# One triangular inverse for both halves of a macro step: 128 partitions on VectorE instead of 64 on VectorE and 64 on GpSimd

## The chip, the core and the metric

The kernel runs on one core of a Trainium2 chip. The metric is the device time of one execution in microseconds (us), as the median of several runs. Engines are named as the profile names them: PE (TensorE matmul), PEld (its weight load), DVE (VectorE), ACT (ScalarE), POOL (GpSimd), SP (SyncE, which issues most DMAs).

## The reference

One encoder layer is applied to a group of 512 tokens and a group of 1024 tokens: a SwiGLU feed-forward, a mixer, a second SwiGLU feed-forward, each with RMS norms and modulation. The mixer is half a pooling mixer and half a two-directional RWKV-7 scan:

```python
def swiglu(h, w1, w3, w2):
    return (jax.nn.silu(h @ w1) * (h @ w3)) @ w2
...
    def step(S, inp):
        r_t, w_t, k_t, v_t, na_t, b_t = inp
        sa = jnp.einsum('bhvk,bhk->bhv', S, na_t)
        S = S * w_t[:, :, None, :] + sa[..., None] * b_t[:, :, None, :] + v_t[..., None] * k_t[:, :, None, :]
        y = jnp.einsum('bhvk,bhk->bhv', S, r_t)
        return S, y
...
    z = h @ w_in
    m = jnp.concatenate([pool_mixer(zp, pool_w, pool_scale),
                         rwkv7_mixer(zr, w0, w2, a0, a2, g2, k_k, k_a, r_k, lnx_g, lnx_b)], axis=-1)
    m = m.astype(x.dtype) @ w_out
```

There are 8 heads of 64 and two directions. `sa` makes each token depend on the tokens before it, so a chunk of 64 tokens needs the inverse of a unit triangular 64x64 matrix.

## The kernel before, in words

**Main stream.** Tokens go in three blocks of 512. Every large product is made of float32r matmuls of 128x128 by 128x512 on a high and a low half of both operands, three matmuls for one product (`mm3`, line 739: `whi` with `hh`, `whi` with `hl`, `wlo` with `hh`). These 11520 matmuls are called dense below. ACT makes `whi` from the loaded weights, POOL (or DVE, by a rule on how busy they are) makes `wlo` (`WStream.split`, line 495). DVE adds the partial outputs of a feed-forward (`y<-y,y`, line 905). After a feed-forward or an output product, `post_gen` (line 771) and `prenorm` (line 658) run on DVE, ACT and POOL before the same block's next dense matmuls can start. The order of the stages is `mainA`, `mainB`, `mainC` (line 1513).

**Scan.** The heads go in pairs. A macro step (12 in all) covers, for one pair, two halves `gi` = 0 and 1; a half holds 4 chunks of 64 tokens in each of 2 directions for 2 heads, so 16 matrices of 64x64. The macro steps 0 to 7 are of the large group, 8 to 11 of the small one. Four kinds of generators run beside the main stream:

- `scan_prep` (line 1158) makes a half's operands, group after group: tanh and exponentials, the products `AR` and `cs` (BK), transposes, and the matrices `MU` (written by two `mask` multiplications a direction, line 1274). Before it writes a half's `AR` it waits until the state of that half of the last macro step is through (line 1248). It then sets `("ba", m, gi)`.
- `scan_inv` (line 1283) inverts the 16 matrices of a half. Their 32x32 diagonal blocks are turned by two transposes so that a partition holds the rows of one parity of one block (`Tin` below: `XN<-MU`), which takes 64 partitions for a half. A chain of 62 dependent multiply and add operations (`XN<-XN`, lines 1307 to 1309) inverts them, on DVE for half 0 and on POOL for half 1 (line 1292). Two transposes put them back (`Tout`: `MU<-XN`), a third copies a block (`Txg`: `MU<-MU`), all on DVE. The off-diagonal block comes from the join: 16 matmuls of 32x32 into PSUM, a copy on ACT, 16 more and another copy (lines 1318 to 1326). The profile counts each of these matmuls twice. A token, `take("inv")`, lets one half in at a time.
- `scan_state` (line 1331), one for each direction, goes through the 8 chunks of a macro step once `("inv", m, gi)` is set for their half; a chunk is three visits to PE with ACT, POOL (`s0p`) and DVE (`SBD`) between.
- `scan_post` (line 1398) normalises the outputs and writes the mixer's half of `m`.

**What sets the order.** All of it is emitted by `run_until` (line 217), a planner that keeps an estimated clock for each engine (`Estimate`, line 42, with a fixed cost for each kind of operation), asks the generator of lowest `prio` that is ready (inverse and preparation -0.5, state 0, post 0.8, main stream 3), and so writes one fixed sequence for each engine. On the chip each engine goes through its own sequence in order: PE waits where an operand is later than the planner thought. The output product of block 0 needs all macro steps of the large group (`("m", 1)`); the output products of blocks 1 and 2 stand in the second feed-forward of block 0, before its chunk 7 (`OUT_AT`, line 934), and need all macro steps.

Nearly all instructions carry line 161, the recorder's, so the profile is read by tiles.

Of the kernel before, what the change touches and what calls it, by code (L numbers as in the profile page):

```python
# [17 lines left out]
P = 128  # L18
# [4 lines left out]
TB = 512  # L23
# [149 lines left out]
def encoder_kernel(ctx, tc, x_prompt, x_sample, c_prompt, c_sample, ada_w, ada_b, n1_pre, n1_post,  # L173
# [392 lines left out]
    def give(k):  # L566
        held.remove(k)
# [712 lines left out]
            ld = nld  # L1280
            flags.add(("ba", m, gi))

    def scan_inv(sb, gi):


        rows = slice(64 * gi, 64 * gi + 64)
        MA, N0, XS = sb.MA, sb.XN[rows, 0:32, :], sb.XN[rows, 32:48, :]
        tmp = sb.XN[rows, 48:53, :].rearrange("p t s -> p (t s)")
        two = lambda ap: ap.rearrange("p t (a s) -> p t a s", a=2)
        e_ = eyes[rows, 30:31]  # L1290
        eye = bass.AP(tensor=e_.tensor, offset=e_.offset, ap=[list(e_.ap[0]), [-2, 16], [1, 32]])
        E = (V, G)[gi]
        for m in range(len(macros)):
            yield has(("ba", m, gi))
            yield from take("inv")
            U = slice(gi * 16, gi * 16 + 16)
            XG = sb.MU[0:64, 2, U, 0:32]
            diag = [MA[32 * q:32 * q + 32, U, 32 * q:32 * q + 32].rearrange("p u t -> p t u") for q in range(2)]
            S.activation(XS, eye, AF.Copy)
            for q in range(2):  # L1300
                V.transpose(two(N0[32 * q:32 * q + 32]), diag[q].unsqueeze(2).to_broadcast([32, 32, 2, 16]))
            yield WAIT
            for j in range(31, 0, -1):
                lo = j // 2
                k_ = 16 - lo
                t3 = tmp[:, 0:k_ * j].rearrange("p (t s) -> p t s", s=j)
                E.tensor_tensor(t3, N0[:, j:j + 1, 0:j].to_broadcast([64, k_, j]),
                                XS[:, lo:16, j:j + 1].to_broadcast([64, k_, j]), ALU.mult)
                E.tensor_tensor(XS[:, lo:16, 0:j], XS[:, lo:16, 0:j], t3, ALU.add)
                if j % 3 == 1:  # L1310
                    yield CHAIN
            for q in range(2):
                V.transpose(diag[q].rearrange("p (t a) u -> p t a u", a=2), two(XS[32 * q:32 * q + 32]))
            V.transpose(XG[0:32], MA[0:32, U, 0:32])
            yield WAIT
            yield from banks()
            pg = pt([P, TB], "sM", 2, pool=ps)
            for u in range(16):
                mm(pg[32:64, u * 32:u * 32 + 32], MA[0:32, gi * 16 + u, 32:64], XG[0:32, u, :])
            S.activation(XG[32:64], pg[32:64, :].rearrange("p (u i) -> p u i", i=32), AF.Copy)  # L1320
            yield WAIT
            yield from banks()
            pe = pt([P, TB], "sM", 2, pool=ps)
            for u in range(16):
                mm(pe[0:32, u * 32:u * 32 + 32], XG[32:64, u, :], MA[32:64, gi * 16 + u, 32:64])
            S.activation(MA[0:32, U, 32:64], pe[0:32, :].rearrange("p (u i) -> p u i", i=32), AF.Copy)
            yield WAIT
            flags.add(("inv", m, gi))
            give("inv")
# [250 lines left out]
    with tc.tile_pool(name="late", bufs=1, reuse_waits="tile") as lp:  # L1580
        sb = ScanBufs(lp)

        spawn(scan_state(sb, 0), 0)
        spawn(scan_state(sb, 1), 0)
        spawn(scan_inv(sb, 0), PRIO_INV)
        spawn(scan_inv(sb, 1), PRIO_INV)
# [39 lines left out]
```

## Time and profile before

| what | value |
|---|---|
| median of 3 runs | 3867.81 us (3865.55 to 3870.64) |
| the profiled execution | 3878.62 us |
| its span, first to last instruction | 3876.6 us |
| PE busy, mean granted clock | 3649.0 us, 94%; 0.936 |
| DVE / ACT / POOL busy | 1977.2 / 1364.7 / 1704.0 us |
| first and last instruction of an inverse chain | 1210.9 us (DVE), 2775.4 us (POOL) |

The page gives the busy share of each engine in 40 slices, and the clock that was granted to PE (PEclk, 9 is full or nearly). A row of the windows view has the stretch, its length, then for PE, PEld, DVE, ACT and POOL the busy us and the number of instructions, then the granted clock as a share of full, the DMA share and GB/s. A row of the lines view has operation, tiles, shapes and count, then busy us and mean ns, then the idle time of the engine before these instructions and who ended it. A row of the timeline has start, length, operation and, in brackets, the idle time before it and who ended that.

### The profile page before, as it was taken

The page shows a single profiled execution, that of the slowest core. Times are in us where ns is not written, and L with a number is a line of the kernel's source. Part 1 is how long each engine was busy: PE and PEld are TensorE (multiplying, and loading weights), DVE is VectorE, ACT ScalarE, POOL GpSimd, SP SyncE. Part 2 cuts the span into 40 slices and gives each one's busy share as a digit, 9 for nine tenths or more (in the row PEclk, how much of TensorE's full clock was granted, in tenths as well). Part 3 has the DMA queues.
Part 4 walks back from the last instruction along what each step waited for, and adds up shares of the span by engine and source line. Part 5 has one row for each costly group of instructions (what it writes and reads, how often), then busy time and mean ns, then how long its engine had stood idle before and what let it go on. Part 6 is the DMA issues. An engine that isn't in the chain of part 4 may idle for free. (4 is left out here: it accounts for less than half of the span.)

```text
span 3876.6 us, 53921 instructions
## 1 busy us (share of the span) xinstructions
PE 3649.0 (94%) x19579; PEld 2752.9 (71%) x19579; DVE 1977.2 (51%) x3633; ACT 1364.7 (35%) x2592; POOL 1704.0 (44%) x2068
## 2 busy tenths in 40 slices
PE   7999999998999999999889988899999999999998
PEld 4667778876776667666667666566777778877886
DVE  3127352245247557765876676766348632232223
ACT  3324342234444333333334333333234432233222
POOL 2334444442233554355445355445544344444444
PEclk8999999999999989999879787789999999999999
DMA  7655343333443222222324233222245343334332
GB/s 270 238 177 160 98 144 93 98 108 117 128 135 112 63 77 66 74 71 88 120 67 121 84 115 109 88 74 71 64 136 163 102 130 98 95 98 138 94 98 76
DMA packets 557981, 432.11 MB, mean 111 GB/s; under 512 B 27029, under 2 KB 511572, under 8 KB 553620
## 3 DMA queue, kind: packets, MB, share of 16 engines
q1 hardware_dynamic: 524900, 379.90, 32.2%
q10 hardware_dynamic: 32816, 48.78, 4.0%
q8 instruction: 154, 2.52, 0.3%
q14 instruction: 111, 0.91, 0.1%
HBM read 367.23 MB, written 61.34 MB: 111 GB/s over the span
## 5 line engine op out<-in xcount | busy, mean ns | idle before, releaser
L161 POOL TENSOR_TENSOR wlo<-wraw,whi 128x512 fp32r<-128x512 f32 x863 | 1146.3, 1343 | 1778.1 <-ACT whi L161 1259.2
L161 DVE TENSOR_TENSOR y<-y,y 128x512 f32<-128x512 f32 x480 | 327.8, 685 | 870.5 <-PE y L161 869.3
L161 ACT ACTIVATE whi<-wraw 128x512 fp32r<-128x512 f32 x938 | 559.6, 622 | 185.5 <-PE v L161 136.9
L161 PE MATMUL u<-hh,whi 128*128 128x512 f32 x1392 | 571.0, 410 | 12.6 <-ACT hh L161 4.4
L161 PE MATMUL v<-hh,whi 128*128 128x512 f32 x1392 | 571.8, 411 | 8.3 <-ACT zraw L161 4.2
L161 PE MATMUL u<-hl,whi 128*128 128x512 f32 x1392 | 568.0, 408 | 12.1 <-DVE hl L161 10.9
L161 PE MATMUL v<-hl,whi 128*128 128x512 f32 x1392 | 568.6, 408 | 5.1 <-DVE hl L161 5.1
L161 PE MATMUL v<-hh,wlo 128*128 128x512 f32 x1392 | 571.1, 410 | 0.0
L161 PE MATMUL u<-hh,wlo 128*128 128x512 f32 x1392 | 569.8, 409 | 0.1
L161 PE MATMUL y<-gh,whi 128*128 128x512 f32 x1056 | 429.2, 406 | 12.0 <-DVE y L161 10.5
L161 PE MATMUL y<-gl,whi 128*128 128x512 f32 x1056 | 426.9, 404 | 0.0
L161 PE MATMUL y<-gh,wlo 128*128 128x512 f32 x1056 | 425.6, 403 | 0.0
L161 POOL TENSOR_TENSOR XN<-XN 64x126 f32<-64x126 f32 (+22 forms) x744 | 311.3, 418 | 66.1 <-DVE XN L161 8.1
L161 PEld LDWEIGHTS u<-hl,whi 128*128 128x128 f32 x1392 | 268.6, 193 | 83.7 <-DVE hl L161 17.9
L161 PEld LDWEIGHTS u<-hh,whi 128*128 128x128 f32 x1392 | 268.4, 193 | 82.6 <-issue 8.3
L161 PEld LDWEIGHTS v<-hh,whi 128*128 128x128 f32 x1392 | 269.8, 194 | 76.4 <-ACT hh L161 7.1
L161 PEld LDWEIGHTS v<-hl,whi 128*128 128x128 f32 x1392 | 270.1, 194 | 72.5 <-DVE hl L161 8.8
L161 PEld LDWEIGHTS u<-hh,wlo 128*128 128x128 f32 x1392 | 268.9, 193 | 69.6 <-issue 10.1
L161 PEld LDWEIGHTS v<-hh,wlo 128*128 128x128 f32 x1392 | 270.0, 194 | 67.3 <-issue 5.9
L161 ACT ACTIVATE gh<-s 128x512 fp32r<-128x512 f32 x132 | 83.3, 631 | 636.7 <-DVE s L161 636.4
L161 PEld LDWEIGHTS y<-gh,whi 128*128 128x128 f32 x1056 | 202.3, 192 | 67.1 <-DVE y L161 11.7
L161 DVE TENSOR_TENSOR XN<-XN 64x126 f32<-64x126 f32 (+22 forms) x744 | 233.2, 313 | 23.8
(252 smaller groups left out, 4456.3 us busy)
## 6 DMA issues: line engine op xcount, KB each, us to landing
wraw<-in_f_w_dram SPq DMA_DIRECT2D x792, 256.0 KB
ada<-in_ada_w_dram SPq DMA_DIRECT2D x32, 1024.0 KB
wraw<-in_w_in_dram SPq DMA_DIRECT2D x98, 256.0 KB
xk<-xs ACTq DMA_DIRECT2D x96, 256.0 KB
xs<-y ACTq DMA_DIRECT2D x48, 256.0 KB
wraw<-in_w_out_dram SPq DMA_DIRECT2D x48, 256.0 KB
in_k<-zk SPq DMA_DIRECT2D x48, 128.0 KB
in_kk<-zkk SPq DMA_DIRECT2D x48, 128.0 KB
```

Source lines behind the costliest of these rows:

```text
L161: return f(*args, **kw)
```

## The change

`scan_inv` becomes one generator for both halves. Half 0's input transposes are issued when half 0 is prepared, half 1's when half 1 is; one chain of 62 operations then runs on all 128 partitions on DVE; six transposes follow; the joins of both halves are issued together, and each half's flag is set behind its second set of matmuls. The token is gone. The number of instructions of the chain on DVE stays 744 (now of 128 partitions), POOL loses its 744, and PE's matmuls are the same.

```diff
-    def scan_inv(sb, gi):
-        rows = slice(64 * gi, 64 * gi + 64)
+    def scan_inv(sb):
...
-        E = (V, G)[gi]
...
         for m in range(len(macros)):
-            yield has(("ba", m, gi))
-            yield from take("inv")
+            yield has(("ba", m, 0))
             S.activation(XS, eye, AF.Copy)
-            for q in range(2):
-                V.transpose(two(N0[32 * q:32 * q + 32]), diag[q].unsqueeze(2).to_broadcast([32, 32, 2, 16]))
+            for gi in range(2):
+                yield has(("ba", m, gi))
+                for q in range(2):
+                    V.transpose(two(N0[quad(gi, q)]), diag[gi][q].unsqueeze(2).to_broadcast([32, 32, 2, 16]))
             yield WAIT
             for j in range(31, 0, -1):
...
-                E.tensor_tensor(t3, N0[:, j:j + 1, 0:j].to_broadcast([64, k_, j]),
-                                XS[:, lo:16, j:j + 1].to_broadcast([64, k_, j]), ALU.mult)
-                E.tensor_tensor(XS[:, lo:16, 0:j], XS[:, lo:16, 0:j], t3, ALU.add)
+                V.tensor_tensor(t3, N0[:, j:j + 1, 0:j].to_broadcast([P, k_, j]),
+                                XS[:, lo:16, j:j + 1].to_broadcast([P, k_, j]), ALU.mult)
+                V.tensor_tensor(XS[:, lo:16, 0:j], XS[:, lo:16, 0:j], t3, ALU.add)
...
+            for gi in range(2):
+                for q in range(2):
+                    V.transpose(diag[gi][q].rearrange("p (t a) u -> p t a u", a=2), two(XS[quad(gi, q)]))
+                V.transpose(XG[gi][0:32], MA[0:32, U[gi], 0:32])
             yield WAIT
-            yield from banks()
-            pg = pt([P, TB], "sM", 2, pool=ps)
+            yield from banks(2)
+            pj = [pt([P, TB], "sM", 2, pool=ps) for gi in range(2)]
+            for gi, pg in enumerate(pj):
...
             yield WAIT
-            yield from banks()
-            pe = pt([P, TB], "sM", 2, pool=ps)
+            for gi, pe in enumerate(pj):
...
+                yield CHAIN
+                flags.add(("inv", m, gi))
```

The planner's sequences move with it. On PE before, in the first feed-forward of block 2 at macro step 1, this is the join of half 0 (`sM<-MU` rows; `u` and `y` rows are dense, `in_wa` rows belong to the preparation of a later group):

```order
L161 MATMUL u_10801<-hl_8857,whi_10662 128x512
L161 MATMUL sM_10863<-MU_9075 32x32 x16
L161 MATMUL u_10801<-hh_8856,wlo_10663 128x512
L161 MATMUL u_10801<-hh_8856,whi_10662 128x512
L161 MATMUL u_10801<-hl_8857,whi_10662 128x512
L161 MATMUL u_10801<-hh_8856,wlo_10663 128x512
L161 MATMUL sM_10888<-in_wa_10767,w2s_151 128x256
L161 MATMUL sM_10889<-in_wa_10767,w2s_151 128x256
L161 MATMUL y_10894<-gh_10423,whi_10724 128x512
L161 MATMUL sM_10896<-MU_9075 32x32 x16
```

A second such join, of half 1, follows 226 rows later. On PE now, at macro step 1 of the same feed-forward, the first matmuls of both halves stand next to each other:

```order
L161 MATMUL v_11104<-hh_8728,whi_11031 128x512
L161 MATMUL sM_11106<-MU_9075 32x32 x16
L161 MATMUL sM_11107<-MU_9075 32x32 x16
L161 MATMUL v_11104<-hl_8729,whi_11031 128x512
L161 MATMUL v_11104<-hh_8728,wlo_11032 128x512
L161 MATMUL v_11104<-hh_8728,whi_11031 128x512
L161 MATMUL v_11104<-hl_8729,whi_11031 128x512
L161 MATMUL v_11104<-hh_8728,wlo_11032 128x512
L161 MATMUL v_11104<-hh_8728,whi_11031 128x512
L161 MATMUL sM_11106<-MU_9075 32x32 x16
```

Half 1's second set stands four rows further on, and the state of the macro step begins right behind it: two places a macro step at which PE meets a join, where there were four.

On DVE before, this is the end of half 0's chain at macro step 1 (`XN<-XN`), its transposes back, and then the preparation of half 1 and half 1's input transposes:

```order
L161 TENSOR_TENSOR XN_9076<-XN_9076 64x16 x2
L161 TENSOR_TENSOR y_9330<-y_9330,y_10748 128x512
L161 TENSOR_TENSOR s_10615<-s_10615,v_10623 128x512
L161 TENSOR_TENSOR gl_10792<-s_10615,gh_10791 128x512
L161 STREAM_TRANSPOSE MU_9075<-XN_9076 32x32x16 x2
L161 STREAM_TRANSPOSE MU_9075<-MU_9075 32x16x32
L161 TENSOR_TENSOR wlo_10836<-wraw_10621,whi_10835 128x512
L161 TENSOR_TENSOR MU_9075<-sM_10846,mask_88 128x4x2x64
L161 TENSOR_TENSOR MU_9075<-sM_10847,mask_88 128x4x2x64
L161 TENSOR_TENSOR y_9330<-y_9330,y_10841 128x512
L161 STREAM_TRANSPOSE XN_9076<-MU_9075 32x1024 x2
```

On DVE now, the end of the one chain of macro step 1; both halves' six transposes stand together and the state's `SBD` follows:

```order
L161 TENSOR_TENSOR XN_9076<-XN_9076 128x16 x2
L161 TENSOR_TENSOR y_9330<-y_9330,y_11012 128x512
L161 TENSOR_TENSOR s_10941<-s_10941,v_10949 128x512
L161 TENSOR_TENSOR gl_11028<-s_10941,gh_11027 128x512
L161 STREAM_TRANSPOSE MU_9075<-XN_9076 32x32x16 x2
L161 STREAM_TRANSPOSE MU_9075<-MU_9075 32x16x32
L161 STREAM_TRANSPOSE MU_9075<-XN_9076 32x32x16 x2
L161 STREAM_TRANSPOSE MU_9075<-MU_9075 32x16x32
L161 TENSOR_TENSOR y_9330<-y_9330,y_11074 128x512
L161 TENSOR_TENSOR y_9330<-y_9330,y_11088 128x512
L161 SCALAR_TENSOR_TENSOR SBD_9077<-sb_9080,PL_9079,s0p_11189 64x64 x2
```

Before, the chain's rows had `SBD` rows of the state between them; now the state's rows stand in front of the chain and behind it.

More of the change, by code (lines that the diff above doesn't have):

```diff
@@ L1281, in scan_prep @@
             flags.add(("ba", m, gi))
-    def scan_inv(sb, gi):
-        rows = slice(64 * gi, 64 * gi + 64)
-        MA, N0, XS = sb.MA, sb.XN[rows, 0:32, :], sb.XN[rows, 32:48, :]
-        tmp = sb.XN[rows, 48:53, :].rearrange("p t s -> p (t s)")
+    def scan_inv(sb):
+        MA, N0, XS = sb.MA, sb.XN[:, 0:32, :], sb.XN[:, 32:48, :]
+        tmp = sb.XN[:, 48:53, :].rearrange("p t s -> p (t s)")
         two = lambda ap: ap.rearrange("p t (a s) -> p t a s", a=2)
-        e_ = eyes[rows, 30:31]
+        e_ = eyes[:, 30:31]
         eye = bass.AP(tensor=e_.tensor, offset=e_.offset, ap=[list(e_.ap[0]), [-2, 16], [1, 32]])
-        E = (V, G)[gi]
-        for m in range(len(macros)):
-            yield has(("ba", m, gi))
-            yield from take("inv")
-            U = slice(gi * 16, gi * 16 + 16)
-            XG = sb.MU[0:64, 2, U, 0:32]
-            diag = [MA[32 * q:32 * q + 32, U, 32 * q:32 * q + 32].rearrange("p u t -> p t u") for q in range(2)]
+        U = [slice(gi * 16, gi * 16 + 16) for gi in range(2)]
+        XG = [sb.MU[0:64, 2, U[gi], 0:32] for gi in range(2)]
+        diag = [[MA[32 * q:32 * q + 32, U[gi], 32 * q:32 * q + 32].rearrange("p u t -> p t u") for q in range(2)]
+                for gi in range(2)]
+        quad = lambda gi, q: slice(64 * gi + 32 * q, 64 * gi + 32 * q + 32)
+        for m in range(len(macros)):
+            yield has(("ba", m, 0))
             S.activation(XS, eye, AF.Copy)
-            for q in range(2):
-                V.transpose(two(N0[32 * q:32 * q + 32]), diag[q].unsqueeze(2).to_broadcast([32, 32, 2, 16]))
+            for gi in range(2):
+                yield has(("ba", m, gi))
+                for q in range(2):
+                    V.transpose(two(N0[quad(gi, q)]), diag[gi][q].unsqueeze(2).to_broadcast([32, 32, 2, 16]))
             yield WAIT
@@ L1310, in scan_inv @@
+                V.tensor_tensor(XS[:, lo:16, 0:j], XS[:, lo:16, 0:j], t3, ALU.add)
                 if j % 3 == 1:
                     yield CHAIN
-            for q in range(2):
-                V.transpose(diag[q].rearrange("p (t a) u -> p t a u", a=2), two(XS[32 * q:32 * q + 32]))
-            V.transpose(XG[0:32], MA[0:32, U, 0:32])
+            for gi in range(2):
+                for q in range(2):
+                    V.transpose(diag[gi][q].rearrange("p (t a) u -> p t a u", a=2), two(XS[quad(gi, q)]))
+                V.transpose(XG[gi][0:32], MA[0:32, U[gi], 0:32])
@@ L1326, in scan_inv @@
[L1326 to L1329, printed above, removed]
+            yield from banks(2)
+            pj = [pt([P, TB], "sM", 2, pool=ps) for gi in range(2)]
+            for gi, pg in enumerate(pj):
+                for u in range(16):
+                    mm(pg[32:64, u * 32:u * 32 + 32], MA[0:32, gi * 16 + u, 32:64], XG[gi][0:32, u, :])
+                S.activation(XG[gi][32:64], pg[32:64, :].rearrange("p (u i) -> p u i", i=32), AF.Copy)
@@ L1331, in scan_state @@
+            yield WAIT
+            for gi, pe in enumerate(pj):
+                for u in range(16):
+                    mm(pe[0:32, u * 32:u * 32 + 32], XG[gi][32:64, u, :], MA[32:64, gi * 16 + u, 32:64])
+                S.activation(MA[0:32, U[gi], 32:64], pe[0:32, :].rearrange("p (u i) -> p u i", i=32), AF.Copy)
+                yield CHAIN
+                flags.add(("inv", m, gi))
     def scan_state(sb, d):
```

8 lines of the change are left out of this document (1 added, 7 removed).

## The prediction

> **What bounds the kernel now.** I read the page first, then the windows view by stage, then the waits of PE, then the timeline around the joins, and last the lines view for the prices.
>
> ```profile
> PE 3649.0 (94%) x19579; PEld 2752.9 (71%) x19579; DVE 1977.2 (51%) x3633; ACT 1364.7 (35%) x2592; POOL 1704.0 (44%) x2068
> ```
>
> PE is the bound: no other engine is busy for more than half of the span. The time is PE's work, plus its idle time, plus what it loses to a lowered clock. The windows view gives the last two by stage (the last row is a stretch of the second feed-forward without scan):
>
> ```profile
> 1200.00:1900.00 700.00, 659.59 (x4471) 473.35 (x4471) 475.48 (x1010) 243.03 (x522) 337.38 (x539) 0.92 0.26 76
> 1900.00:2520.00 620.00, 550.76 (x3653) 390.95 (x3651) 436.63 (x935) 235.34 (x512) 299.92 (x509) 0.79 0.34 103
> 2520.00:2880.00 360.00, 345.98 (x2264) 256.06 (x2263) 199.78 (x409) 118.38 (x255) 170.11 (x254) 0.94 0.27 81
> 3550.00:3850.00 300.00, 299.80 (x1313) 244.87 (x1312) 75.35 (x112) 84.42 (x148) 135.90 (x107) 1.00 0.31 91
> ```
>
> Without the scan PE takes 300 / 1313 = 0.2285 us for a dense matmul, at full clock and with no idle time. With it, in the three upper stretches, PE is idle for 40 + 69 + 14 = 123 us, and loses 700 x 0.08 + 620 x 0.21 + 360 x 0.06 = 208 us to the clock. The matmuls are the same before and after, so the change can only act on these 331 us.
>
> Who makes PE wait there (us in total, times, longest, from 1200 to 3000 us):
>
> ```profile
> PE sM L161 <- DVE MU L161: 42.7, 24, 4.1
> PE sb L161 <- DVE SBD L161: 16.3, 14, 3.7
> PE sM L161 <- DVE ms L161: 5.8, 1, 5.8
> ```
>
> The first is mostly the joins, which wait for the transposes behind the inverse chain; the third is one more join (at 2134.57 us). Together I count 48.5 us for 24 joins. The timeline of PE at two of them, half 0 (chain on DVE), then half 1 (chain on POOL):
>
> ```profile
> 1368.83 0.39 PE L161 MATMUL u<-hl,whi 128*128 128x512 f32 x1
> 1370.65 1.19 PE L161 MATMUL sM<-MU 32*32 32x32 f32 x32 [1.44 <-DVE MU L161]
> ...
> 1444.24 0.39 PE L161 MATMUL u<-hh,whi 128*128 128x512 f32 x1
> 1447.83 1.83 PE L161 MATMUL sM<-MU 32*32 32x32 f32 x32 [3.21 <-DVE MU L161]
> 1449.60 0.80 PE L161 MATMUL u<-hl,whi 128*128 128x512 f32 x1
> ```
>
> Half 0's join waits 1.44 us, half 1's 3.21 us, and the dense matmul behind the second takes 0.80 us where it took 0.39: the clock has dropped. The windows that start at a join's wait price that:
>
> ```profile
> 1312.00:1330.00 18.00, 14.90 (x106) 11.17 (x105) 11.34 (x14) 4.18 (x10) 9.97 (x13) 0.72 0.17 47
> 1369.00:1400.00 31.00, 29.56 (x175) 19.97 (x175) 13.63 (x22) 10.39 (x23) 11.66 (x23) 0.61 0.18 51
> 1444.00:1460.00 16.00, 12.79 (x95) 9.64 (x93) 10.35 (x11) 6.88 (x11) 7.72 (x11) 0.68 0.21 63
> 1564.00:1580.00 16.00, 12.34 (x94) 9.63 (x94) 7.24 (x10) 4.24 (x7) 5.16 (x8) 0.68 0.18 50
> 1629.00:1640.00 11.00, 9.72 (x95) 6.28 (x93) 5.31 (x8) 5.34 (x11) 2.03 (x2) 0.84 0.28 83
> 1702.00:1715.00 13.00, 9.07 (x87) 6.88 (x87) 11.11 (x12) 6.38 (x11) 7.76 (x11) 0.87 0.31 91
> 2128.00:2170.00 42.00, 35.47 (x222) 24.21 (x221) 23.73 (x64) 11.13 (x26) 10.42 (x22) 0.59 0.20 57
> ```
>
> Length times missing clock is 5.0, 12.1, 5.1, 5.1, 1.8 and 1.7 us for six joins of steps 0 to 3; a seventh between them (at 1500 us) waited for nothing, and I give it 0. That is 30.8 / 7 = 4.4 us a join. The last row follows the longest wait, 5.8 us, and lost 17.2 us. So the 24 joins cost 48.5 + 24 x 4.4 = 154 us now.
>
> **The change part by part.** *The chain.* Its price on each engine, from the page, and of the work around it on DVE, from the lines view by shape (1200 to 2850 us):
>
> ```profile
> L161 POOL TENSOR_TENSOR XN<-XN 64x126 f32<-64x126 f32 (+22 forms) x744 | 311.3, 418 | 66.1 <-DVE XN L161 8.1
> L161 DVE TENSOR_TENSOR XN<-XN 64x126 f32<-64x126 f32 (+22 forms) x744 | 233.2, 313 | 23.8
> ```
>
> ```profile
> L161 DVE STREAM_TRANSPOSE XN<-MU 32x1024 f32<-32x1024 f32 x48 | 94.1, 1961 | 0.7
> L161 DVE SCALAR_TENSOR_TENSOR SBD<-sb,PL,s0p 64x64 f32<-64x64 f32 x320 | 90.5, 283 | 172.4 <-PE sb L161 146.2 <-POOL XN L161 16.5 <-POOL s0p L161 4.2
> L161 DVE TENSOR_TENSOR y<-y,y 128x512 f32<-128x512 f32 x112 | 75.8, 681 | 79.1 <-PE y L161 78.3
> L161 DVE TENSOR_TENSOR MU<-sM,mask 128x512 f32<-128x512 f32 x96 | 61.4, 679 | 22.9 <-PE sM L161 22.8
> L161 DVE TENSOR_TENSOR wlo<-wraw,whi 128x512 fp32r<-128x512 f32 x63 | 58.2, 927 | 44.8 <-ACT whi L161 44.2 <-DMA in_wa<-za 0.3
> L161 DVE STREAM_TRANSPOSE MU<-XN 32x512 f32<-32x512 f32 x48 | 51.0, 1063 | 28.4 <-POOL XN L161 27.3
> L161 DVE TENSOR_TENSOR_SCAN cs<-rst,sg 128x256 f32<-128x256 f32 x46 | 39.0, 889 | 0.8
> L161 DVE TENSOR_TENSOR cs<-in_wa,sg 128x256 f32<-128x256 f32 x46 | 31.0, 674 | 1.3 <-POOL in_wa L161 1.3
> L161 DVE SCALAR_TENSOR_TENSOR cs<-ta,sg 128x256 f32<-128x256 f32 x46 | 29.4, 639 | 22.2 <-PE sM L161 21.8
> L161 DVE TENSOR_TENSOR gl<-s,gh 128x512 fp32r<-128x512 f32 x32 | 23.3, 728 | 24.7 <-ACT gh L161 24.7
> L161 DVE TENSOR_TENSOR s<-s,v 128x512 f32<-128x512 f32 x32 | 21.8, 680 | 6.0 <-PE v L161 5.9
> L161 DVE SCALAR_TENSOR_TENSOR ta<-ta,in_kk 128x512 f32<-128x512 f32 x23 | 20.0, 868 | 10.6 <-POOL in_wa L161 10.6
> L161 DVE STREAM_TRANSPOSE MU<-MU 32x512 f32<-32x512 f32 x24 | 16.8, 700 | 0.7
> L161 DVE TENSOR_SCALAR sg<-sg 128x512 f32<-128x512 f32 x23 | 11.9, 518 | 2.6 <-ACT sg L161 2.5
> L161 DVE SCALAR_TENSOR_TENSOR bq<-in_wa,vB,in_r 128x256 f32<-128x256 f32 x22 | 11.4, 558 | 0.0
> ```
>
> POOL loses 311 us, which is worth nothing by itself: POOL is not the bound. DVE keeps 744 chain operations. The trace has none on 128 partitions with these widths; if they cost double they would add 233 us of DVE, if the width of partitions is free, nothing. I take nothing: the nearest row, `y<-y,y` on 128 partitions with 512 elements, takes 681 ns, and the chain's operations have 136 elements at most.
>
> *The join's wait, where the sum is decided.* The one chain of a step starts only when half 1 is prepared, and its join must be covered by dense matmuls. The order of the changed kernel has, at step 1, between the last `sM<-AR` row of the preparation and the first `sM<-MU` row, 166 dense matmuls and four short ones (`in_wa`, 256 wide; an estimate of 0.3 us each, below the 0.39 us of a row of 512): 166 x 0.2285 + 1.3 = 39.2 us of cover. On DVE the same stretch holds 2 `mask`, 2 input transposes, 62 chain operations, 8 `y<-y,y`, 2 scans, one each of the `cs`, `ta`, `sg`, `wlo` rows and 2 `bq`, 2 `s` and 2 `gl`, then 4 transposes back and 2 copies: 1.4 + 3.9 + 19.4 + 5.4 + 1.8 + (0.7 + 0.6 + 0.9 + 0.5 + 0.9) + 1.1 + 1.4 + 1.5 + 4.3 + 1.4 = 45.2 us; with the chain's own gaps, 23.8 / 12 = 2.0 us, 47.2 us. So PE comes 8.0 us early. Half 0's set may go when half 0's copy is done, 2 x 1.06 + 0.70 = 2.8 us before half 1's; it fills 1.2 us (the x32 row), and 6.8 us of idle time remain. Half 0's join of step 1 now tells how sure that is: its wait of 1.44 us came after a stretch that had lost 5.0 us to the clock (1312 to 1330), so at full clock it would have been 6.4 us. Part of such a loss will stay, so I take 5.5 us a step, between 1.4 (half 0's join as it is) and 8.0.
>
> *The clock behind it.* It lies between 5.1 us (behind 3.2 us of wait) and 17.2 (behind 5.8); I take 8, nearer to the end where most of the rows lie. So 12 joins cost 12 x (5.5 + 8) = 162 us where 24 cost 154: **+8 us**.
>
> *The state.* No chain stands between its `SBD` rows any more, so the planner sets its 8 chunks close: at step 1 the order has 50 dense matmuls from the first to the last `XN` row of the state, where the two halves have 65 and 56 now. That is 50 / 8 x 0.2285 = 1.4 us of cover a chunk instead of 3.5. The preparation's `AR`, `cs` and `mask` stand between those `SBD` rows on DVE, and PE's next visit waits for that. The total of that wait is 16.3 us now. It could go (no chain in front on DVE or POOL) or grow by 4 us a step; I take 1 us a step, **+12 us**.
>
> *The two stalls between blocks.* At 1900 to 2000 and 2400 to 2500 us PE waits for `post_gen` and `prenorm`, which need DVE:
>
> ```profile
> 1900.00:2000.00 100.00, 81.68 (x535) 57.64 (x532) 76.88 (x142) 41.12 (x84) 56.55 (x96) 0.66 0.35 107
> 2400.00:2500.00 100.00, 82.39 (x545) 58.23 (x545) 77.20 (x177) 38.31 (x86) 43.69 (x56) 0.74 0.35 111
> ```
>
> By the order the first gets a whole chain into it on DVE (62 operations, 0 now) and loses 14 `SBD`; the second loses 42 chain operations and gets 6 `SBD`. At 313 and 283 ns that is +19.4 - 4.0 and -13.1 + 1.7: **+4 us**, with 15 us to either side since DVE is three quarters busy there.
>
> *The ends of the scan.* From join to join a step has 258, 250, 273 and 272 dense matmuls now, and 285, 286, 290 and 239 then. The scan's last state row moves from dense matmul 7270 to 7366; the first that needs all of it is number 7536, and 170 x 0.2285 = 39 us are left for the last `scan_post` and the loads: nothing on the path, with a thin margin.
>
> The sum is 8 + 12 + 4 = +24 us on the profiled execution's 3878.6 us. The median of the runs lies 10.8 us under that, so I forecast 3867.8 + 24 = **3892 us**.
>
> **The rivals.** *The join's wait stays as short as half 0's is now (faster).* For it: the covers of steps 0 and 2 are longer, 173 and 188 dense matmuls, and the chain has fewer transposes of others behind it. With 3 us of wait and 4.4 of clock a step, 12 x 7.4 = 89 us replace 154, -65; with the state's +4 and the stalls' +4 that is 3811 us, and up to 3860 for half of it. It decides at a DVE path of 42 us from the last `mask` to the last copy; against it stands the sum of 45.2. Chance 0.27.
>
> *Gain and loss cancel.* Fewer joins, each dearer, within 7.7 us of the median, 0.2%, which is about what a measurement of this kernel can tell from no change. Chance 0.16, 3868 us.
>
> *The scan ends too late (slower still).* If the step takes 5 us more than the order's dense matmuls say, the scan's end comes 12 x 5 = 60 us later against a margin of 39 us, and the main stream stands for 20 us: 3892 + 20 = 3912 us. Chance 0.10, as the wait at the joins holds the main stream back as well. *Half 0's joins cost no clock now (slower still).* If the lost clock behind them (12.1 and 1.8 us) has another cause and only waits of 3 us and more drop it, the joins cost now 48.5 us and, for half 1 alone, 12 x (5.0 + 5.1 + 5.1 + 1.7) / 4 = 51 us: 99 us in place of 154. The change then costs 55 us more than the sum, 3947 us. For it: the waits of half 1 are the long ones. Against it: the 1369 row has a clock of 0.61 behind a wait of 1.44 us. Chance 0.05. [...]
>
> That the change does not do what it says is excluded by the order: POOL has no `XN` row left, DVE 744 on 128 partitions.
>
> **How the numbers follow.** The forecast has 0.42, the late end 0.10, the free joins of half 0 0.05, all slower by over 0.2%: 0.57. The same 0.16, faster 0.27. The ends of the unknown costs, 12 x (7.5 + 10) = 210 us of joins above and 12 x (3.5 + 5) = 102 below, put the sum at +72 and -36. Between the cases the range is 3835 to 3932: about one in ten is left out below, the deepest of the faster cases, and one in ten above.
>
> **What would show it.** In the changed profile PE's wait `sM <- DVE MU` should come about 12 to 24 times, with 5 us a step in place of 4, and the windows at the joins should have a clock of 0.6 to 0.75 for 10 to 25 us. The chain's mean on DVE should stay near 313 ns. PE's wait for `SBD` should grow from 16 to about 28 us. The first stall should be longer, the second shorter. I am wrong if the wait at the join is below 3 us, if PE's idle time between 1200 and 2880 us falls below 100 us, or if the chain's operations cost more on 128 partitions.

## The result and the profile after

| kernel | median of the runs | ratio to before |
|---|---|---|
| before | 3869.22 us (3865.55 to 3874.38, 4 runs) | 1 |
| changed | 4063.82 us (4048.80 to 4078.34, 4 runs) | 1.0502 (95% interval 1.0461 to 1.0542) |

The change makes the kernel 195 us slower. The prediction had 24 us and a range that ended at 3932 us: the sign was right, the size was not. The profiled execution of the changed kernel took 4064.57 us, with a span of 4062.8 us and a mean granted clock of 0.907 (0.936 before).

The first row of the page, after:

```profile
PE 3741.8 (92%) x19579; PEld 2809.2 (69%) x19579; DVE 1997.7 (49%) x3599; ACT 1362.2 (34%) x2582; POOL 1441.8 (35%) x1358
```

PE is busy 93 us longer (3649.0 before) with the same 19579 matmuls, and idle for 321 us of the span where it was idle for 228. So half of the loss is idle time, and half is the same work at a lower clock. POOL has lost its chain; DVE's busy time has hardly changed.

The windows view of after. The first three stretches hold about the dense matmuls that 1200 to 1900, 1900 to 2520 and 2520 to 2880 us held before; the last is the stretch without scan:

```profile
1200.00:1940.00 740.00, 672.03 (x4364) 485.20 (x4364) 466.30 (x911) 235.73 (x505) 226.25 (x237) 0.87 0.24 71
1940.00:2605.00 665.00, 555.34 (x3485) 390.11 (x3485) 414.43 (x910) 226.42 (x487) 185.25 (x225) 0.77 0.32 96
2605.00:3068.00 463.00, 423.45 (x2563) 307.06 (x2560) 249.36 (x501) 130.55 (x284) 132.52 (x131) 0.82 0.22 65
3738.00:4038.00 300.00, 299.81 (x1318) 245.57 (x1317) 75.63 (x112) 84.70 (x148) 136.41 (x107) 1.00 0.31 91
```

The three stretches have grown by 40, 45 and 103 us, which is nearly all of the loss, and the stretch without scan is as it was. The third also holds 299 more matmuls, scan work that the first two held before, so its 103 us are not all lost there. PE's idle time in them is 68 + 110 + 40 = 218 us (123 before). Length times missing clock is 96 + 153 + 83 = 332 us (208 before).

Who makes PE wait there, after:

```profile
PE sM L161 <- DVE MU L161: 46.4, 35, 6.2
PE y L161 <- DVE y L161: 46.0, 16, 11.6
PE y L161 <- DVE acc L161: 27.0, 3, 18.1
PE sb L161 <- DVE SBD L161: 15.5, 11, 2.0
```

and two rows of the same view of before:

```profile
PE y L161 <- DVE y L161: 4.6, 2, 2.7
PE y L161 <- DVE acc L161: 3.5, 3, 1.8
```

The row `sM <- DVE MU` is about what it was, 46.4 us against 42.7, but the joins' part of it is smaller; the rest stands before matmuls of other tiles. The tile view of `MU` has the idle time of PE before the matmuls on `MU` (us, times) that DVE's `MU` ended, by my count all of it at joins, before and then after:

```profile
DVE MU L161: 36.4, 17
```

```profile
DVE MU L161: 24.2, 15
```

With the joins that other operations ended, PE waits 47.8 us at the joins before and 24.2 after. The wait for `SBD` is about as it was, 15.5 us against 16.3. What is new is PE waiting for DVE's `y` and `acc`. The `y` rows are dense matmuls that stand ahead of the join and need a PSUM buffer that DVE has not added up yet. The timeline of DVE at one of them shows why:

```profile
1567.69 1.37 DVE L161 TENSOR_TENSOR wlo<-wraw,whi 128x512 fp32r<-128x512 f32 x1 [0.35 <-ACT whi L161]
1568.99 5.88 DVE L161 TENSOR_TENSOR XN<-XN 128x135 f32<-128x135 f32 x6
1574.79 1.28 DVE L161 TENSOR_TENSOR y<-y,y 128x512 f32<-128x512 f32 x2
```

and the timeline of PE at the same place:

```profile
1575.62 0.77 PE L161 MATMUL y<-gh,whi 128*128 128x512 f32 x1 [4.48 <-DVE y L161]
```

Beside the chain's operations POOL makes `wlo` in these 7 us:

```profile
1567.22 6.84 POOL L161 TENSOR_TENSOR wlo<-wraw,whi 128x512 fp32r<-128x512 f32 x5 [4.92 <-ACT whi L161]
```

Six operations of the chain take 5.88 us, the `y<-y,y` behind them comes late, and PE stands for 4.48 us. The longest single wait is in the first stall between blocks, where DVE's norm operations (`acc`) have 26 operations of the chain among them, 9.4 us:

```profile
1978.12 4.64 DVE L161 TENSOR_TENSOR XN<-XN 128x31 f32<-128x31 f32 x14
1987.11 1.76 DVE L161 TENSOR_TENSOR XN<-XN 128x96 f32<-128x96 f32 x6
1991.73 3.00 DVE L161 TENSOR_TENSOR XN<-XN 128x126 f32<-128x126 f32 x6
```

```profile
1995.38 1.86 PE L161 MATMUL y<-ones,acc 128*128 128x1 f32 x8 [18.14 <-DVE acc L161]
```

The chain's group on the page has become dearer by 77 ns an operation (233.2 us, 313 ns before):

```profile
L161 DVE TENSOR_TENSOR XN<-XN 128x126 f32<-128x126 f32 (+22 forms) x744 | 290.4, 390 | 22.5
```

To place the loss I counted over all records of the two traces. A chain window goes from a chain's first operation on DVE to 9 us behind its last (transposes and joins); a state phase holds the state's copies on ACT that follow each other within 12 us.

| | before | after |
|---|---|---|
| PE idle in the 12 chain windows | 41.9 us | 152.8 us |
| PE idle in the rest of the scan / outside the scan | 79.6 / 87.9 us | 60.7 / 90.1 us |
| clock lost in the chain windows (while PE is busy) | 51.6 us (48.7) | 93.7 us (55.9) |
| clock lost in the state phases (while PE is busy) | 106.2 us (95.3) | 197.4 us (195.0) |
| length of the state phases, dense matmuls in them | 823 us, 1367 | 814 us, 773 |

Idle time counts as far as it lies in a window; clock lost is length times missing clock. (The expectations below say 135 us for PE's idle time: they leave out the wait of 18.14 us, which begins 0.9 us ahead of a chain window.) All of the new idle time lies in the chain windows. Part of it is idle time that lay elsewhere before: 31.6 us stand in the window at the first stall (4.7 before), while the stretch without a dense matmul at that stall has only grown from 33.7 to 36.7 us. Clock that is missing while PE is idle costs nothing more, so the figures in brackets count: nearly all of the new loss of clock, 100 us, lies in the state phases, where PE hardly waits, and 7 us in the chain windows. PE's busy time grew by 93 us. Four state phases in a row of before, each of one half, from the windows view:

```profile
1327.00:1353.00 26.00, 26.00 (x190) 17.16 (x188) 21.73 (x59) 8.52 (x24) 9.37 (x13) 1.00 0.15 42
1381.00:1418.00 37.00, 37.00 (x218) 25.91 (x217) 11.30 (x25) 11.54 (x29) 19.07 (x39) 0.79 0.12 36
1459.00:1491.00 32.00, 31.01 (x219) 21.43 (x219) 28.65 (x76) 8.26 (x23) 8.81 (x11) 1.00 0.20 59
1507.00:1543.00 36.00, 34.55 (x228) 24.35 (x228) 23.01 (x36) 14.55 (x34) 25.24 (x47) 0.95 0.20 59
```

and the first four of after, each of both halves:

```profile
1304.00:1377.00 73.00, 71.09 (x425) 45.84 (x424) 25.45 (x53) 19.94 (x53) 15.27 (x22) 0.65 0.12 36
1452.00:1516.00 64.00, 62.87 (x448) 42.21 (x449) 29.82 (x67) 18.91 (x52) 15.37 (x21) 0.81 0.21 63
1599.00:1654.00 55.00, 53.05 (x406) 34.30 (x406) 23.36 (x50) 17.49 (x51) 12.65 (x21) 0.85 0.15 44
1735.00:1799.00 64.00, 62.86 (x450) 42.19 (x450) 29.82 (x67) 18.84 (x51) 15.31 (x20) 0.81 0.20 62
```

PE is busy for 96 to 98% of each of the four phases of after, and yet has a clock of 0.65 to 0.85. Before, one of the four has a low clock, the one behind a join's wait that the prediction showed (at 1369 us).

### The profile page after: what moved, and what is told of

Its sections match the earlier page's. It is cut to its first block, busy times and chain, and to the rows that moved or that the text cites. A ratio compares the mean times of both kernels' runs of the same rounds, so it can differ in the third digit from the quotient of the medians.

```text
span 4062.8 us, 53210 instructions
## 1 busy us (share of the span) xinstructions
PE 3741.8 (92%) x19579; PEld 2809.2 (69%) x19579; DVE 1997.7 (49%) x3599; ACT 1362.2 (34%) x2582; POOL 1441.8 (35%) x1358
## 5 line engine op out<-in xcount | busy, mean ns | idle before, releaser
L161 POOL TENSOR_TENSOR wlo<-wraw,whi 128x512 fp32r<-128x512 f32 x891 | 1179.5, 1340 | 1959.4 <-ACT whi L161 1485.8
L161 PE MATMUL u<-hh,whi 128*128 128x512 f32 x1392 | 577.2, 415 | 24.2 <-ACT hh L161 10.8
L161 PE MATMUL y<-gh,whi 128*128 128x512 f32 x1056 | 437.9, 415 | 58.2 <-DVE y L161 52.9
L161 DVE TENSOR_TENSOR XN<-XN 128x126 f32<-128x126 f32 (+22 forms) x744 | 290.4, 390 | 22.5
L161 PEld LDWEIGHTS y<-gh,wlo 128*128 128x128 f32 x1056 | 205.6, 195 | 49.1 <-issue 3.6
```

Source lines behind the costliest of these rows:

```text
L161: return f(*args, **kw)
```

## The experiments

The theory after the result (A): the loss has two causes. First, the chain's path on DVE is longer than the prediction had it and delays the `y` additions and the norms in the same queue, so PE is idle. Second, the state's chunks, set close, run at a low clock. The rivals: the waits alone cause all of it (B); the engine that the chain moved to (C); the planner's wrong prices, so that the change is sound with right ones (D).

| run | median, us | ratio to before, 95% interval | PE idle in chain windows | lost in state phases |
|---|---|---|---|---|
| changed kernel | 4063.8 | 1.0502 (1.0461 to 1.0542) | 152.8 | 197.4 |
| short chain | 3992.0 | 1.0307 (1.0271 to 1.0343) | 107.9 | 187.9 |
| wlo on ACT | 3896.2 | 1.0063 (1.0043 to 1.0082) | 79.9 | 172.0 |
| before, both chains on DVE | 3917.1 | 1.0119 (1.0089 to 1.0149) | (24 chains) | 112.8 |
| state spread | 4017.2 | 1.0371 (1.0334 to 1.0408) | 146.0 | 133.4 |
| before, wlo on ACT | 3710.7 | 0.9586 (0.9551 to 0.9621) | 26.1 | 76.0 |
| before, state spread | 3843.0 | 0.9918 (0.9888 to 0.9948) | 52.1 | 72.9 |
| before, no token | 3889.0 | 1.0044 (1.0027 to 1.0061) | 66.0 | 123.9 |
| merged, two engines | 4117.7 | 1.0625 (1.0591 to 1.0660) | 207.2 | 156.2 |
| short transposes | 4030.9 | 1.0411 (1.0381 to 1.0441) | 140.6 | 178.7 |
| changed, costs mended | 3947.1 | 1.0193 (1.0162 to 1.0224) | 117.2 | 156.7 |
| before, costs mended | 3818.5 | 0.9869 (0.9852 to 0.9887) | 53.1 | 94.1 |
| before, costs and spread | 3839.8 | 0.9918 (0.9891 to 0.9946) | 57.7 | 112.3 |

The last two columns are counted from each run's trace as in the table above (the lost clock whether PE is busy or not); the profiled execution of the changed kernel with `wlo` on ACT lies 21 us under its median, that with mended costs 21 us above. The kernel before had medians of 3869 to 3875 us beside the several runs; differences in us to it are taken against the one beside.

**The chain made short.**

```diff
-                V.tensor_tensor(t3, N0[:, j:j + 1, 0:j]..., XS[:, lo:16, j:j + 1]..., ALU.mult)
+                est.op("V", "tensor_tensor", sx, {})
+                nc.vector.tensor_tensor(t3[:, 0:1, 0:1], N0[:, j:j + 1, 0:1], XS[:, lo:lo + 1, j:j + 1], ALU.mult)
```

(and the addition likewise; the planner is told the full sizes, so the order stays.)

> The changed kernel in its own order on every engine, but each of the 744 chain operations handles one element a partition, so that a chain takes about 4 us of DVE instead of 24.2 (the blocks are not inverted). Theory A (two causes: the chain's long path on DVE makes PE idle, and the state's chunks, set close, lower the clock by themselves): PE's idle time falls by the 93 us that the change added, the clock lost in the chains' windows by about 40, and the clock lost in the state phases stays near 197 us; about 3930 us. Rival B (the chain's waits cause all of it, the low clock in the state too): the state phases' loss falls to the 106 us of the kernel before, 3870 us or less. Rival C (the chain is not it: the serial structure, its transposes and joins are): above 4000 us.

It took 3992 us. A chain of one element an operation is not 4 us long; its rows in the lines view (minimum, median and maximum in ns):

```profile
L1310 DVE TENSOR_TENSOR XN<-XN x372: 127/159/1274, 1242.1 to 2889.4; 128x1 f32<-128x1 f32 x186
L1313 DVE TENSOR_TENSOR XN<-XN x372: 158/159/1292, 1242.3 to 2889.6; 128x1 f32<-128x1 f32 x186
```

Most operations take about 159 ns, whatever their width would have been, and some still take 1.3 us: a chain takes 17.5 us by my sum, 6.7 less than 24.2. So 12 x 6.7 = 81 us less on DVE were worth 72 us: 0.89 us for each. A's figure of 3930 us was missed, since it had a chain of 4 us. PE's idle time in the chain windows fell by 45 us, and the loss in the state phases hardly moved (197.4 to 187.9), as A has it and B not.

**What makes an operation of the chain take 1.3 us.**

```diff
-                E.tensor_tensor(wl, t, wh.bitcast(F32), ALU.subtract)
+                if E is G:
+                    est.op("G", "tensor_tensor", (wl, t, wh.bitcast(F32)), {})
+                    nc.scalar.activation(wl, t, AF.Copy)
+                else:
+                    E.tensor_tensor(wl, t, wh.bitcast(F32), ALU.subtract)
```

> The changed kernel in its own order, but the wlo operations that POOL did are issued on ACT as copies (wlo then holds the weights themselves, not their low halves). The theory that POOL's wlo operations hold up the chain on DVE: the mean of a chain operation falls from 390 ns to 250 to 270, a chain from 24.2 to about 16 us, and with 8 us less a step PE's idle time falls by 60 to 95 us; 3960 to 4000 us. The rival, that the operations are slow for another reason (128 partitions, the other work on DVE): the mean stays near 390 ns and the time at 4064 us or above, since ACT has some 440 us more to do.

> The control for the run with wlo on ACT: the kernel before in its own order, with the wlo operations that POOL did issued on ACT as copies (wlo then holds the weights themselves). In the changed kernel the same edit was worth 168 us. If POOL's wlo operations cost the changed kernel more than the kernel before, because all of its chain work stands in front of PE in one run, the gain here is well below that: 40 to 90 us, 3780 to 3830 us. If they cost both kernels alike, the gain is 140 us or more, 3730 us or less, and they are no part of what the change does.

In the changed kernel the edit is worth 168 us, and a chain falls from 24.2 to 17.5 us. In the kernel before it is worth 164 us, so the expected difference between the two was wrong: POOL's `wlo` operations hold DVE up in both kernels alike, and the change costs 3896.2 - 3710.7 = 185 us without them. They are a large cost of this kernel, and next to none of the cost of the change. Chain operations of over 1 us fall from 93 to 14 in the changed kernel and from 40 to 5 in the kernel before. The pages of the two runs, changed first:

```profile
PE 3678.0 (95%) x19579; PEld 2776.0 (72%) x19579; DVE 1737.5 (45%) x3599; ACT 1807.9 (47%) x3473; POOL 262.5 (7%) x467
```

```profile
PE 3566.1 (96%) x19579; PEld 2705.0 (73%) x19579; DVE 1761.6 (47%) x3633; ACT 1794.1 (48%) x3455; POOL 564.9 (15%) x1205
```

DVE's busy time falls by 260 and 216 us with the same instructions. Even so PE stays busy for 112 us more in the changed kernel than in the kernel before.

**The engine or the merging.** In one run the kernel before gets both chains on DVE, one half at a time:

```diff
-        E = (V, G)[gi]
+        E = V
```

In another the changed kernel keeps its order on PE but splits the chain as before, the upper 64 partitions on POOL:

```diff
+                for h, eng in enumerate((nc.vector, nc.gpsimd)):
+                    hr = slice(64 * h, 64 * h + 64)
+                    eng.tensor_tensor(t3[hr], N0[hr, j:j + 1, 0:j]..., XS[hr, lo:16, j:j + 1]..., ALU.mult)
+                    eng.tensor_tensor(XS[hr, lo:16, 0:j], XS[hr, lo:16, 0:j], t3[hr], ALU.add)
```

> The kernel before with half 1's chain on DVE as well, 64 partitions each, one half at a time as before; the order follows. If the load on DVE is what costs (24 chains of 19 us instead of 12): DVE gains 233 us and PE's idle time grows by 24 x 7.7 - 43 = 140 us, 4000 us or more. If the joining of both halves into one serial run is what costs: half 1's chain is the faster on DVE, the state of one half still runs beside the inverse of the other, and the time stays between 3830 and 3920 us.

> The changed kernel in its own order on PE, with one run for both halves, but the chain's 62 operations are issued twice, on partitions 0 to 63 on DVE and on 64 to 127 on POOL, side by side. If joining both halves into one serial run is what costs, and the engine is not: the time stays at 4000 us or more. If the move of half 1's chain from POOL to DVE is what costs, it falls to 3870 to 3920 us. With two chains that hold each other up (as the last run's first theory has it) it becomes longer than the changed kernel's, 4080 to 4200 us.

Twice the chains on DVE, unmerged, cost 1.2% (44 us), although DVE has 231 us more to do:

```profile
L161 DVE TENSOR_TENSOR XN<-XN 64x126 f32<-64x126 f32 (+22 forms) x1488 | 509.5, 342 | 48.0
```

So rival C has at most 44 of the 195 us, and with twice the number of chains on DVE that the changed kernel has. The rest goes with one run for both halves. Merged on two engines the kernel takes 4118 us, 54 more than the changed one; this run alone doesn't tell the engine from the merging, since its chain on DVE has become longer with POOL's chain beside it. The median of an operation is 426 to 432 ns (274 in the changed kernel):

```profile
L1314 DVE TENSOR_TENSOR XN<-XN x372: 172/426/1404, 1239.8 to 3006.2; 64x126 f32<-64x126 f32 x18, 64x30 f32<-64x30 f32 x12, 64x56 f32<-64x56 f32 x12, 64x78 f32<-64x78 f32 x12
L1316 DVE TENSOR_TENSOR XN<-XN x372: 177/432/1411, 1240.0 to 3006.4; 64x126 f32<-64x126 f32 x18, 64x30 f32<-64x30 f32 x12, 64x56 f32<-64x56 f32 x12, 64x78 f32<-64x78 f32 x12
```

One thing here speaks against a simple form of A: PE has the changed kernel's own order, with the same 773 dense matmuls in the state phases, and yet loses 156.2 us there instead of 197.4. The number of dense matmuls alone doesn't set that loss.

In a third the kernel before loses the token:

```diff
-            yield from take("inv")
...
-            give("inv")
```

> The kernel before without the token: half 0's chain on DVE and half 1's on POOL may run at the same time; the order follows. If an operation of POOL holds up one of DVE that reads two operands from SBUF, the operations of the DVE chain that meet POOL's chain get dearer by 0.2 to 0.4 us each, and the mean of the DVE chain rises from 313 ns to 400 or more; 3860 to 3950 us. If only the large wlo operations do it, the mean stays near 313 ns, and the scan, which in the order ends 232 dense matmuls earlier, gives 3840 to 3870 us.

Without the token the two chains of the kernel before overlap only in part; the mean rose to 340 ns, between the two theories, and the time by 0.4%. The run alone decides nothing; the split run shows that POOL's chain holds up DVE's (a median of 426 to 432 ns for each of its operations, 274 without).

**The state.** The planner lets the state's next visit wait longer, 400 ns in the changed kernel and 500 in the kernel before:

```diff
-AFTER_STATE = 200
+AFTER_STATE = 400
```

> The changed kernel with AFTER_STATE 400 instead of 200, so that the planner sets the state's visits further apart, with more dense matmuls between them; its scan ends 58 dense matmuls later. Theory A (closely set chunks lower the clock): the loss in the state phases falls from 197 us toward 140, and part of it is given back where block 0 waits for the eighth macro step; 4010 to 4050 us. Rival B (the clock is low because of the waits at the chain): the loss in the state phases stays within 20 us of 197, and the time is 4064 us or more.

> The kernel before with AFTER_STATE 500 instead of 200: the state's visits are set further apart, with more dense matmuls between them. If closely set chunks lower the clock by themselves, the loss of 106 us in its state phases falls to 70 to 90 us and the time to 3840 to 3865 us. If in the kernel before the clock is lost to the waits at the joins alone, the loss stays at 100 us or more and the time at 3868 us or above, since the state of each half is through later.

Both became faster, by 47 and 32 us, and in both the loss in the state phases fell by as much or more (197.4 to 133.4, 106.2 to 72.9), while PE's idle time rose a little (303.6 to 312.6, 209.4 to 210.8 by my count over all gaps). So dense matmuls between the chunks are worth clock: A, and not B alone. In the changed kernel part was given back as expected: PE goes 119 us without a dense matmul before block 0's output product, 50 us in the changed kernel.

**The path on DVE.** Half 1's two input transposes made narrow, from the second macro step on:

```diff
-                    V.transpose(two(N0[quad(gi, q)]), diag[gi][q]...)
+                    if gi == 0 or m == 0:
+                        V.transpose(*tx)
+                    else:
+                        est.op("V", "transpose", tx, {})
+                        nc.vector.transpose(tx[0][:, 0:1], tx[1][:, 0:1])
```

> The changed kernel in its own order, but half 1's two input transposes, which stand between half 1's last mask multiplication and the chain, handle one column instead of 32 from the second macro step on (half 1's inverses are then of stale blocks): about 3.6 us less on DVE in each of 11 macro steps. If every microsecond on DVE between half 1's preparation and the joins costs PE about 0.9 us, as the run with the short chain has it: 11 x 3.6 x 0.9 = 36 us less, 4015 to 4040 us. If only the chain's own operations matter, because other work of DVE stands between them: less than 15 us, 4050 us or more.

22 transposes became shorter, from 1.95 to 0.225 us, 38 us in all, and the time fell by 33: 0.87 us for each. The four runs of the changed kernel lie 30 us apart, so this figure is rough; with the short chain's 0.89 it puts the price of a microsecond on DVE between half 1's preparation and the joins at about 0.9 us. It isn't paid at one place: PE's idle time fell by 13 us only (303.6 to 290.3, nearly all of it in the chain windows, 152.8 to 140.6), the rest came back as clock. The narrow ones in the lines view:

```profile
L1307 DVE STREAM_TRANSPOSE XN<-MU x22: 221/225/229, 1380.9 to 2886.9; 32x32 f32<-32x32 f32 x22
```

**The planner's prices.**

```diff
             cost = 65 + 1.04 * n + (60 if name == "scalar_tensor_tensor" else 0)
+            if name == "transpose":
+                cost = 65 + 1.9 * n
...
+                est.free["V"] += 100.0
                 V.tensor_tensor(t3, N0[:, j:j + 1, 0:j]...)
+                est.free["V"] += 100.0
                 V.tensor_tensor(XS[:, lo:16, 0:j], XS[:, lo:16, 0:j], t3, ALU.add)
```

> The changed kernel, with the planner's costs brought nearer to the trace: 65 + 1.9 ns an element for a transpose on DVE, and 100 ns more for each pair of chain operations. In the order the joins come later, but the macro step gets longer: the scan ends 80 dense matmuls later, the stretch without dense matmuls before block 0's output product has 150 rows where it had 82, and 503 instead of 650 dense matmuls stand between neighbouring chunks of the state. Theory A (the serial macro step is what costs; the cover for the chain is taken from the state, whose clock falls): PE's idle time in the chains' windows falls from 135 to below 100 us, but the loss in the state phases stays at 190 us or more and the time at 4020 to 4090 us. The rival (the planner's wrong prices are the cause, so that the change is sound with the right ones): 3950 us or less.

> The control for the run with the planner's costs mended: the kernel before with the same prices (65 + 1.9 ns an element for a transpose on DVE, 100 ns more for each operation of the chain on DVE). In the order the joins come later, and the stretch without dense matmuls before block 0's output product has 150 rows, as in the changed kernel with the same prices. If the wrong prices hurt the changed kernel more, because a whole chain with ten transposes stands between half 1's preparation and its joins: the gain here is small, and the longer stretch takes it back, 3830 to 3900 us. If they hurt both alike: 117 us as there, 3780 us or less.

(The first text says 100 ns for each pair of operations; in the kernel that ran it is 100 ns for each operation, as the diff shows.) The changed kernel gains 117 us, which is the number that rival D named, and the loss in the state phases did not stay at 190 us, although the dense matmuls in them did not become more (732 against 773). But the kernel before gains too, 51 us (1.3%), so the change still costs 3947.1 - 3818.5 = 129 us with the same prices in both. D has a third of the loss, 66 of 195 us; the rest is the change's own. Where it lies now: PE goes 116 us without a dense matmul while block 0's output product waits for the eighth macro step (98 us in the kernel before with these prices), as the windows view of the changed kernel with mended costs has it,

```profile
2289.00:2405.00 116.00, 78.19 (x609) 57.76 (x609) 66.19 (x171) 23.87 (x65) 20.24 (x29) 0.54 0.18 53
```

and in their traces, which lie 150 us apart, PE is idle for 64 us more in the chain windows than in the kernel before with the same prices (117.2 and 53.1; 26 of the 64 us are one wait in that stretch), and loses 63 us more of clock in the state phases (156.7 and 94.1).

The last run has the mended prices and `AFTER_STATE = 500` together in the kernel before:

> The kernel before with both edits that made it faster: the planner's mended prices, and AFTER_STATE 500. If the two gains are of different kinds (waits at the chain; clock in the state), they add up in part: the loss in the state phases falls from 94 us toward 70, and the time to 3785 to 3810 us. The rival: both lengthen the macro step, and what one gives the stretch before block 0's output product takes back; 3815 to 3850 us.

The rival had the time right: the two gains don't add up. Its reason is not what the traces show. The loss in the state phases rose to 112 us, which no run explains, and the stretch before block 0's output product did not get longer (94 us without a dense matmul, 98 without the spread). The fastest kernel of the study is the one before with the mended prices, 3818 us.

## Why the prediction was wrong, point by point

**What bounds the kernel** was right: PE, with the same matmuls, loses idle time and clock in the scan, and the loss outside the scan did not change. The 331 us were no limit, since the change adds to them, and they count clock that is missing while PE is idle twice.

**Width.** Right: the sum of each chain operation's fastest record is 15.2 us a chain on 64 partitions and 15.7 on 128.

**The chain's price** (19.4 us, from 313 ns) was taken over from the kernel before. It was 24.2 us. The 313 ns were no property of the operation, but of what POOL did beside it: by my count 63 of the 744 operations met a `wlo` of POOL before and 98 after, at 610 and 822 ns extra each; with `wlo` off POOL the mean of the kernel before is 261 ns, that of the changed one 282. Why more of them meet in the changed kernel, no run tells. It is not the main cause of the loss: with `wlo` off POOL in both kernels the chain takes 17.5 us against 16.2, and the change still costs 185 us.

**The join's wait** (5.5 us a step) failed: it was looked for at the wrong place. At the join itself PE waits 24.2 us in all, 2.0 a step. But the step weighed the dense matmuls ahead of the join as cover that runs by itself; the `y` matmuls among them need DVE, whose queue holds the chain, and they stop first, as do the norms. In the chain windows PE is idle for 152.8 us, 12.7 a step, where the sum had 5.5. At 0.9 us for each microsecond of the path, the 4.8 us by which the chain was priced too low would be 12 x 4.8 x 0.9 = 52 us in the changed kernel, an estimate.

**The clock behind the joins** (12 x 8 = 96 us) agrees with 93.7 us in the chain windows by luck: 38 of these lie where PE is idle. While PE is busy the chain windows lose 55.9 us, 7 more than before. The prediction's windows at the joins, which start with the wait, count the same way.

**The state** (12 us, as waits for `SBD`) is the step that failed most. That wait did not grow (15.5 us), but the phases lost 91 us more of clock, 100 us more while PE is busy, which is as much as PE's busy time grew (93 us). The step asked what a chunk waits for, and not what clock the chunk's small matmuls run at when only 1.4 us of dense matmuls stand between. Before, one half's state ran while the other half's chain was under way, so that the same dense matmuls covered both; in the changed kernel preparation, chain and state follow each other, and each dense matmul covers one thing. The traces show it: before, the state phases lie beside a chain for 626 of their 823 us, in the changed kernel for none; and they hold 1367 dense matmuls before, 773 after, over the same 820 us. The runs with the state spread confirm that dense matmuls there are worth clock; the split run, with 773 of them and 156.2 us lost, shows that their number doesn't settle it.

**The stalls between blocks** (+15.4 and -11.4) had the right signs: from dense matmul 5800 to 6000 the time went from 168 to 177 us, from 6570 to 6600 from 75 to 60. From 6380 to 6400 it went from 68 to 79, which the step did not have; the three make +5 where it had +4, so the sum agrees by luck. (The faster rival's 3860 us is a slip of its own: half of 65 us with 8 us against it gives 3843.)

**The ends of the scan** cost nothing at the last one, as said: the lag behind the kernel before is 188 us at dense matmul 7400 and stays there. The other end, the large group's before block 0's output product, was not weighed. In the changed kernel it costs little (50.0 us without a dense matmul, 46.7 before), but it takes back what the mended prices and the spread state would have given.

**What would show it** named PE's wait for `SBD` and the chain's mean; both came out otherwise, the chain's mean for reasons other than its 128 partitions. Of the signs of being wrong, the wait at the join came: 2.0 us a step, below 3, and it did not mean a faster kernel.

What stays open: whether a low clock in a state phase needs a gap to begin with, and how the 195 us divide exactly, since the causes don't add up one by one. The last section says what the traces show; no run took the gaps away and left the state as it is.

## What to carry to other kernels

Two half-size stages that overlap can share one piece of cover; merged into one they need it one after the other, so count what each dense matmul covers before and after, not the number of joins. When a chain is put into an in-order queue, look for everything behind it in that queue that the bound engine needs, not only for the chain's own consumer. And price an operation by its fastest record and what runs beside it, since its mean moves when the neighbour's work does (390 to 282 ns here when `wlo` left POOL).

## What the runs showed of the hardware

**The clock has a memory.** One wait in the timeline of the changed kernel's PE, and the windows around and behind it:

```profile
1485.14 1.02 PE L161 MATMUL sM<-bones,psq 128*128 128x2 f32 x8 [1.11 <-DVE MU L161]
```

```profile
1484.00:1488.00 4.00, 2.89 (x22) 2.36 (x22) 3.70 (x15) 0.66 (x2) 0.77 (x2) 0.97 0.45 130
1488.00:1512.00 24.00, 24.00 (x130) 16.28 (x131) 15.41 (x27) 5.48 (x15) 7.69 (x7) 0.51 0.25 77
```

After 1.11 us of idle time the clock drops to half and stays there for 24 us in which PE is never idle. The same phase of the changed kernel with mended prices, with 466 matmuls where the window above of 1452 to 1516 us has 448, keeps the full clock:

```profile
1434.00:1491.00 57.00, 56.98 (x466) 39.00 (x465) 29.47 (x69) 18.68 (x53) 17.27 (x22) 1.00 0.25 77
```

The traces give the clock in steps of 3.41 us, each at full or at half (the 98 stretches of the trace of after are 3.4 to 833 us long). Over the scan in the traces of before, after and the first ten experiments I counted, for each step with under 1 us of idle time in it and the step before, how often the next step was at half clock, by the share of the two steps' time in dense matmuls:

| dense share | from full clock | from half clock |
|---|---|---|
| 0 to 0.2 | 13% of 187 | 86% of 231 |
| 0.2 to 0.4 | 4% of 492 | 91% of 292 |
| 0.4 to 0.6 | 2% of 951 | 84% of 347 |
| 0.6 to 0.8 | 1% of 1029 | 5% of 110 |
| 0.8 to 1 | 0% of 839 | 0% of 25 |

With over 1 us of idle time the full clock was lost in 74% of the steps with a share of 0.2 to 0.4 (136 steps). So in these traces small matmuls keep a full clock (at a dense share of 0.2 to 0.4 it was lost in 4% of the steps) and seldom bring it back: behind a step at half clock the next was at half in 84 to 91% up to a share of 0.6, and in 5% or less above. A busy PE alone did not bring it back in the 1488 row, 24 us at 0.51.

**DVE and POOL hold each other up.** With POOL's chain beside it an operation of DVE's chain has a median of 426 to 432 ns, without 274. The chain's operations, which read both inputs from SBUF, took 610 and 822 ns longer where they met a `wlo` of POOL (63 before, 98 after). `y<-y,y`, which reads one input from PSUM, did not: by my count from 1200 to 3000 us its mean beside a `wlo` is 681 and 675 ns (34 and 17 operations), and with nothing on POOL beside it 679 ns in both traces (54 and 55). In the other direction, a `wlo` of POOL takes 1.29 us in the trace of before where nothing on DVE runs beside it (232 operations), and 1.36 us on average, up to 2.65 us, where something does (631). The 216 to 260 us that DVE won when `wlo` left POOL agree; so do the six operations of the 1568.99 row, 0.98 us each beside `wlo` operations of 1.37.

**A floor for short operations.** In the run with the short chain, the chain's operations on DVE, with one element a partition, take 159 ns (median), so 62 dependent ones take some 10 us even at that width (62 x 159 ns, an estimate).
